# Turning queries and keys as plain fp32, two heads to a transpose, and splitting them after the turn

## The chip, the cores and the metric

The kernel runs on one core of one Trainium2 chip. The metric is the time of one execution on the device in microseconds (us). Each engine has its own queue of instructions and works it off in order: PE (TensorE) multiplies and transposes, DVE (VectorE), ACT (ScalarE) and POOL (GpSimd) work element by element, SP issues DMAs. PE writes into PSUM, which the other engines read.

## The reference, cut to what matters

512 tokens with 16 meta tokens ahead of them (528 in all, width 1024) pass through two layers. What the change touches is how queries and keys come about and who reads them: queries `q` (8 heads of 64, normalised), one key head `k`, and the same for the indexer, `q_idx` (8 heads of 64) and `k_idx`. The indexer's scores choose 128 keys for each query, and attention runs over those.

```python
def hybrid_layer(x, norm_g, w_in, qn_g, kn_g, ...):
    h = rms_norm(x, norm_g)
    proj = jnp.einsum('btd,de->bte', h, w_in)
    q, k, v, gate_a, u_b, gate_b, q_idx, k_idx, w_idx, merge = jnp.split(proj, ...)
    q = apply_rope(rms_norm(q.reshape(B, T, 8, 64), qn_g), cos_h, sin_h)
    k = apply_rope(rms_norm(k, kn_g), cos, sin)
    q_idx = apply_rope(q_idx.reshape(B, T, 8, 64), cos_h, sin_h)
    k_idx = apply_rope(k_idx, cos, sin)
    attn = indexer_sparse_attention(q, k, v, q_idx, k_idx, w_idx, k_top)
    y_a = jnp.einsum('bte,ed->btd', attn * jax.nn.silu(gate_a), w_a)
    ...                                   # a pooling branch y_b, two gates
    return x + jnp.einsum('btd,de->bte', g_a * y_a + g_b * y_b, w_out)

# indexer_sparse_attention, for one block of 128 queries
    s = jnp.einsum('bqhd,bkd->bqhk', qib, k_idx_f)
    score = jnp.einsum('bqhk,bqh->bqk', jax.nn.relu(s), wib * idx_scale)
    score = jnp.where(visible, score, NEG_INF)
    _, sel = lax.top_k(score, k_top)
    logits = jnp.einsum('bqhd,bqkd->bqhk', qb, gather(k, sel)) * attn_scale
    p = jax.nn.softmax(logits, axis=-1)
    out = jnp.einsum('bqhk,bqkd->bqhd', p, gather(v, sel))
```

## The kernel before, in words

**Precision.** Nearly every matmul keeps fp32's accuracy with operands in PE's faster fp32r format: an operand is split into a high part (the value rounded to fp32r, a CAST of ACT) and a low part (the value minus the high part, a subtraction of DVE), and the products of the parts are added up in PSUM. `hhi`/`hlo` are the split input, `w` holds the split weights. For queries and keys the two parts lie on the two halves of the partitions: `qi` (index queries) and `qq` (queries) are `[128, 4 heads, 128 tokens]` with a head's 64 high rows over (or under) its 64 low rows, and `KI` and `KK` are `[128, 2, 528]` with the key's high part doubled over all 128 partitions at index 0 and its low part at index 1, so that two matmuls (`a<-KI,qi`) give the whole product.

**Tiling.** Tokens are in one block of 16 (the meta tokens, t = 0) and four of 128 (t = 1 to 4). A projection of one token block to 256 columns (four heads) is a group of 24 matmuls 128x256, `tok_group`, into one PSUM bank `d`; it ends with `group_done()`. Two halves of eight heads make `g` = 0 and 1.

**Order.** The order of PE and DVE is the order in which the Python code emits instructions (a manual schedule); that of ACT, POOL and SP is set when the program is built. `later(fn, n)` runs `fn` n groups of PE work on. `half_done()` is called in the middle and at the end of each group and draws filler from generators: index scores (`index_steps`) and attention. A meter keeps estimated times of PE and DVE (`pe_cost`, `dve_cost`) and lets a step of the top-k search (`topk_steps`: 16 rounds of MAX8 and MATCH_REPLACE8 on score tiles `sc`) into DVE's order only when DVE is not ahead of its share; so an added DVE instruction moves the steps of the search to later places.

**PSUM.** Eight banks: three `d` for projections, four `a` for everything short (transposes, index scores, logits), one `v`. A bank is given out again in turn, and its next writer on PE waits until its last reader is done.

**Queries before the change** (`q_post`, 8 blocks of index queries and 8 of queries in each layer): two DVE products from PSUM (`t<-d,...`, L63 is the line of the meter's call, through which every PE and DVE instruction goes), POOL adds them (L677), ACT writes the high parts into `qs` (L686), DVE the low parts beside them (`qs<-t,qs`), PE turns `qs` by four fp32r transposes, one for a head with both parts (`a<-identr,qs`), and ACT copies the bank to `qi` or `qq` in one go (L697). The norm of the queries is applied later, in the softmax. The meta block's queries of layer 0 (t = 0) go the same way and stay as they are.

**Keys before the change** (`kv_post`, 5 blocks in each layer): four DVE products of 64 columns, POOL adds (L633), DVE scales by the norm (`t<-t,rk`), ACT writes the high parts twice into `ks` (L640), DVE the low parts (`ks<-t,ks`), four fp32r transposes, ACT copies to `KK` (L650) and `KI` (L651).

Of the kernel before, what the change touches and what calls it, by code (L numbers as in the profile page):

```python
# [9 lines left out]
F32R = mybir.dt.float32r  # L10
AF = mybir.ActivationFunctionType
OP = mybir.AluOpType
# [16 lines left out]
LB = 6  # L29
PB = 4  # L30
# [11 lines left out]
QN = 2  # L42
R_IDX = 3
UF = 2
QI = 3
# [46 lines left out]
def tile_block(ctx: ExitStack, tc: tile.TileContext, x, meta, w_in, pool_w, w_a, w_b, w_out, rows, hgain, c_tab, out):  # L92
    nc = tc.nc
    act, gp = nc.scalar, nc.gpsimd
    pe, dve = Metered(nc.tensor, pe_cost), Metered(nc.vector, dve_cost)
# [3 lines left out]
    tmp = ctx.enter_context(tc.tile_pool(name="tmp", bufs=2))  # L99
# [3 lines left out]
    def f(ap):  # L103
        return ap.bitcast(F32)
# [3 lines left out]
    def bank(tag, dt=F32):  # L108
        return psum.tile([128, 512], dt, tag=tag, name=tag, bufs=BANKS[tag])
# [229 lines left out]
    pend = deque()  # L339
# [4 lines left out]
    def later(fn, n=2):  # L344
        pend.append((count[0] + n, fn))
# [8 lines left out]
                    fill.popleft()  # L354

    credit = [0.0]

    sel = deque()
    spare, seen, share = [0.0], [0.0, 0.0], [FULL]

    def half_done():
        credit[0] += rate[0] / 2
        n = int(credit[0])
        credit[0] -= n
        pump(n)
# [22 lines left out]
        seen[1] = dve.us  # L388

    def flush():  # L390
        while pend:
            pend.popleft()[1]()

    def drain():
        while fill:
# [56 lines left out]
    KI = {}  # L452
# [151 lines left out]
    def kv_post(l, t, ps):  # L604
        s, m = TOK[t]
        p2 = ps[:m, :256].rearrange("p (g c) -> p g c", g=2)[:, :, 0:64]
        sq = tmp.tile([128, 64], F32, tag="tt", name="sq", bufs=6)
        ss = small(1, "ss")
        act.activation(sq[:m], ps[:m, 0:64], AF.Square, scale=HD ** -0.5, accum_out=ss[:m])
        rk = small(1, "rk")  # L610
        inv_rms(rk[:m], ss[:m])
        t1 = tmp.tile([128, HB], F32, tag="tt", name="t1", bufs=6)
        t2 = tmp.tile([128, HB], F32, tag="tt", name="t2", bufs=6)
        v1 = t1[:m, :128].rearrange("p (g d) -> p g d", g=2)
        for g, (C, S) in enumerate(((Cg, Sg), (ctab, stab))):
            dve.tensor_tensor(v1[:, g], p2[:, g], C[:m, t], op=OP.mult)
            dve.tensor_tensor(t2[:m, 64 * g:64 * g + 64].rearrange("p (a d) -> p a d", a=2),
                              p2[:, g].rearrange("p (a d) -> p a d", a=2)[:, ::-1, :],
                              S[:m, t].rearrange("p (a d) -> p a d", a=2), op=OP.mult)
        if t:  # L620
            act.activation(V[:, t - 1, :], ps[:, 64:128], AF.Copy, scale=0.5)
            act.activation(wab[:, t - 1], ps[:, 192:200], AF.Abs, scale=IDX_SCALE)
            act.activation(wsg[:, t - 1], ps[:, 192:200], AF.Sign, scale=-1.0 if t == 1 else 1.0)
        else:
            act.activation(VM, ps[:m, 64:128], AF.Copy, scale=0.5)

            def meta_values():
                rp = bank("a")
                pe.matmul(rp[:, :64], repl, VM, start=True, stop=True)
                for h in range(NH):  # L630
                    dve.tensor_scalar(BV[:, h // 2, h % 2, :], rp[:, :64], hmask[:, h:h + 1], None, op0=OP.mult)
            later(meta_values, 3)
        gp.tensor_tensor(t1[:m, :128], t1[:m, :128], t2[:m, :128], op=OP.add)  # L633
        ks = tmp.tile([128, 4, 128], F32R, tag="P", name="ks", bufs=PB)
        k4 = ks[:m].rearrange("p (g a) (b d) -> p g a b d", g=2, b=2)
        b1 = v1[:, :, None, :].to_broadcast([m, 2, 2, 64])

        def second():
            dve.tensor_scalar(t1[:m, :64], t1[:m, :64], rk[:m], None, op0=OP.mult)
            act.copy(k4[:, :, 0], b1)  # L640

        def third():
            dve.tensor_sub(k4[:, :, 1], b1, f(k4[:, :, 0]))

        def trans():
            tp = bank("a", F32R)
            for j in range(4):
                pe.transpose(tp[:, j * 128:j * 128 + m], ks[:m, j, :], identr[:m, :m])
            t4 = f(tp).rearrange("p (g j c) -> p g j c", g=2, j=2)
            act.copy(KK[:, :, s:s + m], t4[:, 0, :, :m])  # L650
            act.copy(KI[0][:, :, s:s + m], t4[:, 1, :, :m])  # L651
        later(second, 1)
        later(third, 2)
        later(trans, 4)

    def q_post(t, ps, normed, dst, g=0):
        s, m = TOK[t]
        p3 = ps[:m, :256].rearrange("p (h d) -> p h d", h=4)
        t1 = tmp.tile([128, HB], F32, tag="tt", name="t1", bufs=6)
        t2 = tmp.tile([128, HB], F32, tag="tt", name="t2", bufs=6)  # L660
        v1 = t1[:m, :256].rearrange("p (h d) -> p h d", h=4)
        C, S = (Cg[:m, t], Sg[:m, t]) if normed else (ctab[:m, t], stab[:m, t])
        dve.tensor_tensor(v1, p3, C[:, None, :].to_broadcast([m, 4, 64]), op=OP.mult)
        dve.tensor_tensor(t2[:m, :256].rearrange("p (h a d) -> p h a d", h=4, a=2), swapped(ps[:m, :256], 4),
                          S.rearrange("p (a d) -> p a d", a=2)[:, None, :, :].to_broadcast([m, 4, 2, 32]), op=OP.mult)
        if normed:
            sq = tmp.tile([128, HB], F32, tag="tt", name="sq", bufs=6)
            act.activation(sq[:m, :256], ps[:m, :256], AF.Square, scale=HD ** -0.5)
            ss = small(4, "ss4")
            rq = small(4, "rq")  # L670

        def norms():
            dve.tensor_reduce(ss[:m], sq[:m, :256].rearrange("p (h d) -> p h d", h=4), axis=AX.X, op=OP.add)
            inv_rms(rq[:m] if t == 0 else RQ[:, t - 1, 4 * g:4 * g + 4], ss[:m], gp if l else dve)
        if normed and t == 0:
            norms()
        added[0] = gp.tensor_tensor(t1[:m, :256], t1[:m, :256], t2[:m, :256], op=OP.add).ins  # L677
        if normed:
            qs = tmp.tile([128, 544], F32R, tag="L", name="qs", bufs=LB)[:, :512].rearrange("p (h c) -> p h c", h=4)
        else:  # L680
            qs = tmp.tile([128, 4, 128], F32R, tag="P", name="qs", bufs=PB)

        def second():
            if normed and t == 0:
                dve.tensor_tensor(v1, v1, rq[:m, :, None].to_broadcast([m, 4, 64]), op=OP.mult)
            act.copy(qs[:m, :, 0:64], v1)  # L686
            if normed and t:
                norms()

        def third():  # L690
            dve.tensor_sub(qs[:m, :, 64:128], v1, f(qs[:m, :, 0:64]))

        def trans():
            tp = bank("a", F32R)
            for h in range(4):
                pe.transpose(tp[:, h * 128:h * 128 + m], qs[:m, h, :], identr[:m, :m])
            act.copy(dst, f(tp).rearrange("p (h c) -> p h c", h=4)[:, :, :m])  # L697
        later(second, 1)
        later(third, QN if normed else QI)
        later(trans, QN + 1 + l if normed else QI + 1)  # L700

    SC = {}

    def index_steps(i, g, qS):
        n = NK[i]
        for hh in range(4):
            h = 4 * g + hh
            r = tmp.tile([128, 544], F32, tag="L", name="r", bufs=LB)
            for o, w in KPARTS[i]:
                ps = bank("a")  # L710
                pe.matmul(ps[:, :w], qS[:, hh, :], KI[0][:, 0, o:o + w], start=True, stop=False)
                pe.matmul(ps[:, :w], qS[:, hh, :], KI[0][:, 1, o:o + w], start=False, stop=True)
                e = min(w, n - o)
                act.activation(r[:, n - 1::-1] if i == 0 else r[:, o:o + e], ps[:, :e], AF.Relu,  # L714
                               scale=wab[:, i, h:h + 1])
            later(lambda h=h, r=r: accumulate(i, h, r), 1)
            yield
# [34 lines left out]
    QS = {}  # L752
# [4 lines left out]
    def attention(ensure, later_rate, on):  # L757
        st, pvs, pms, turned = {}, {}, {}, []

        def logits(u):  # L760
            i, j = divmod(u, 4)
            if j == 0:
                ensure(i)
                pms[i] = tmp.tile([128, NH, 16], F32, tag="pm", name="pm")
                if i == 0:
                    gp.tensor_scalar(NR, RQ, -1.0, None, op0=OP.mult)
            st[u] = []
            for hh in range(2):
                h = 2 * j + hh
                qS = QS[i, h // 4][:, h % 4, :]  # L770
                for pi, (o, w) in enumerate(KPARTS[i]):
                    ps = bank("a")
                    pe.matmul(ps[:, :w], qS, KK[:, 0, o:o + w], start=True, stop=False)
                    pe.matmul(ps[:, :w], qS, KK[:, 1, o:o + w], start=False, stop=True)
                    st[u].append((hh, pi, o, w, ps))
# [806 lines left out]
```

## Time and profile before

| | |
|---|---|
| runs (three) | 737.03, 737.45, 738.73 us; median 737.45 |
| span of the profiled execution | 735.6 us |
| around the span, taken as median less span | 1.85 us |
| PE busy | 730.1 us, 99% of the span |
| PE weight loads (overlap PE) | 706.0 us, 96% |
| DVE busy | 586.2 us, 80% |
| ACT busy | 482.1 us, 66% |
| POOL busy | 254.2 us, 35% |

The profiled execution's time is the span, from its first to its last instruction; the runs' times contain what lies around it. The page's forty slices show PE at nine tenths or more in all but the last, at a granted clock of nine tenths or more in all. The rows below have the form: engine and line, operation, output<-inputs by the program's names with buffer numbers left out, shape, count. A timeline's row begins with its start in the span and its length in us; a group's row ends with busy us, mean ns of one, and the idle time just before, with what ended most of it. Matmuls overlap, so the length of a PE row is longer than the time to the next row's start; prices of PE work are taken between starts.

### The profile page before, as it was taken

How to read it: one execution, taken by the hardware profiler on the slowest of the kernel's cores; microseconds unless marked ns; L12 is line 12 of the kernel's file. 1: busy time of each engine (PE TensorE's matmuls, PEld its weight loads, DVE VectorE, ACT ScalarE, POOL GpSimd, SP SyncE). 2: the span in 40 equal slices, each digit the busy share in tenths (PEclk: the TensorE clock that was granted, in tenths of full speed). 3: DMA queues.
4: the chain of work that ended last, by engine and by line, in shares of the span. 5: the costliest groups of instructions: out<-in, count | busy, mean ns of one | idle time of the engine just before them, and what ended most of it. 6: DMA issues, size and time to landing. Idle time of an engine off the chain costs nothing.

```text
span 735.6 us, 16083 instructions
## 1 busy us (share of the span) xinstructions
PE 730.1 (99%) x5949; PEld 706.0 (96%) x5949; DVE 586.2 (80%) x1478; ACT 482.1 (66%) x1099; POOL 254.2 (35%) x336
## 2 busy tenths in 40 slices
PE   9999999999999999999999999999999999999998
PEld 8999998999999999999999989998899999999997
DVE  6966999998997775894348668999989978768874
ACT  6779735757788886543245796357588977775643
POOL 3751174731222211163247411757131231106300
PEclk9999999999999999999999999999999999999999
DMA  8767765964655434643523778659564654438832
GB/s 268 233 172 165 167 145 115 229 149 99 141 119 122 94 84 105 192 141 118 143 89 87 171 175 199 157 116 205 126 156 103 144 115 90 113 107 268 202 88 71
DMA packets 103566, 106.41 MB, mean 145 GB/s; under 512 B 5008, under 2 KB 83632, under 8 KB 103488
## 3 DMA queue, kind: packets, MB, share of 16 engines
q1 hardware_dynamic: 91888, 74.89, 34.5%
q0 software_dynamic: 11520, 30.41, 23.1%
q8 instruction: 46, 0.75, 0.4%
q14 instruction: 32, 0.26, 0.1%
q10 hardware_dynamic: 80, 0.08, 0.0%
HBM read 66.41 MB, written 8.55 MB: 102 GB/s over the span
## 4 chain that ended last, share of the span: by engine, by line
PE 99%; DVE 0%; issue 0%; ACT 0%; DVEq 0%
PE d L63 80%; PE a L63 13%; PE v L63 5%; DVE ot L63 0%; DVE w L63 0%; ACT w L269 0%; ACT osum L1121 0%; DVE idle L63 0%; DVE nf L63 0%; DVE ta L63 0%; DVEq L63 0%; DVE ones L63 0%; ACT p L1021 0%; DVE ss L63 0%; DVE mhalf L63 0%
## 5 line engine op out<-in xcount | busy, mean ns | idle before, releaser
L63 PE MATMUL d<-hhi,w 128*128 128x256 f32 (+3 forms) x1392 | 278.4, 291 | 0.0
L63 PEld LDWEIGHTS d<-hhi,w 128*128 128x128 f32 x1392 | 222.2, 188 | 3.0 <-issue 0.6
L63 PE MATMUL d<-hlo,w 128*128 128x256 f32 (+3 forms) x696 | 189.8, 289 | 0.0
L63 DVE TENSOR_TENSOR w<-raw,w 128x512 fp32r<-128x512 f32 (+1 forms) x156 | 121.5, 785 | 14.0 <-ACT w L269 13.2
L63 PEld LDWEIGHTS d<-hlo,w 128*128 128x128 f32 x696 | 131.3, 189 | 1.4 <-issue 0.2
L63 PE MATMUL d<-hsum,w 128*128 128x264 f32 (+1 forms) x720 | 95.5, 285 | 0.0
L63 PEld LDWEIGHTS d<-hsum,w 128*128 128x128 f32 x720 | 89.6, 188 | 0.7 <-issue 0.3
L63 PE MATMUL d<-w,hhi 128*128 128x256 f32 x576 | 86.1, 287 | 0.0
L269 ACT CAST w<-raw 128x512 fp32r<-128x512 f32 x132 | 79.0, 624 | 6.7 <-DMA raw<-s 5.9
L63 PEld LDWEIGHTS d<-w,hhi 128*128 128x128 f32 x576 | 74.7, 188 | 4.7 <-issue 3.5
L255 POOL DMA_DIRECT2D raw<-raw x22 | 19.9, 905 | 115.5 <-DMA raw<-in_w_in_dram 30.3
L63 DVE MATCH_REPLACE8 sc<-m,sc 128x400 f32<-128x400 f32 (+2 forms) x100 | 54.4, 547 | 0.0
L221 POOL DMA_DIRECT2D w<-raw x34 | 31.8, 951 | 64.1 <-ACT w L220 46.5
L63 DVE MAX8 m<-sc 128x8 f32<-128x400 f32 (+2 forms) x100 | 53.2, 556 | 0.9
L793 ACT ACTIVATE lt<-lt,mn,NR 128x144 f32<-128x144 f32 (+3 forms) x64 | 42.3, 663 | 12.8 <-DVE mn L63 12.8
L284 POOL DMA_DIRECT2D raw<-s x22 | 19.6, 891 | 87.9 <-DVE s L63 40.7
L63 DVE SCALAR_TENSOR_TENSOR sc<-r,wsg,sc 128x144 f32<-128x144 f32 (+3 forms) x56 | 32.4, 582 | 16.9 <-ACT r L714 14.7
L63 PE MATMUL d<-w,hlo 128*128 128x256 f32 x288 | 45.6, 281 | 0.0
L63 PE MATMUL d<-mhi,w 128*128 128x272 f32 (+2 forms) x192 | 45.5, 324 | 0.0
L808 POOL TENSOR_SCALAR pm<-lt,rs 128x16 f32<-128x16 f32 x48 | 26.3, 575 | 44.2 <-DVE rs L63 33.1
L677 POOL TENSOR_TENSOR t<-t,t 128x256 f32<-128x256 f32 (+1 forms) x34 | 32.3, 951 | 25.6 <-DVE t L63 25.2
L1427 POOL TENSOR_TENSOR hlo<-ta,hhi 128x256 fp32r<-128x256 f32 (+1 forms) x28 | 26.8, 965 | 41.6 <-PE d L63 29.4
(247 smaller groups left out, 1564.5 us busy)
## 6 DMA issues: line engine op xcount, KB each, us to landing
raw<-in_w_in_dram SPq DMA_DIRECT2D x88, 256.0 KB, 3.5
w<-raw POOLq DMA_DIRECT2D x34, 512.0 KB, 5.9
raw<-in_w_in_dram SPq DMA_DIRECT2D x32, 512.0 KB, 4.6
raw<-in_w_out_dram SPq DMA_DIRECT2D x12, 512.0 KB, 3.8
raw<-raw POOLq DMA_DIRECT2D x22, 256.0 KB, 4.2
raw<-s POOLq DMA_DIRECT2D x22, 256.0 KB, 3.7
kept<-res SPq DMA_DIRECT2D x16, 264.0 KB, 3.2
res<-kept SPq DMA_DIRECT2D x16, 264.0 KB, 6.2
```

The source lines that it names most:

```text
L63: return fn(*a, **k)
L221: gp.dma_start(t, raws[c][s], accum_op=OP.add)
L255: gp.dma_start(raws[c][0][:, 1], raws[c][0][:, 0], accum_op=OP.add)
L269: act.copy(t[:, 0], blk[src[n]])
L284: gp.dma_start(blk["a12"], blk["s2"], accum_op=OP.add)
L677: added[0] = gp.tensor_tensor(t1[:m, :256], t1[:m, :256], t2[:m, :256], op=OP.add).ins
L793: act.activation(L[hh][:, :n], L[hh][:, :n], AF.Exp, scale=NR[:, i, h:h + 1], bias=mn[:, hh:hh + 1], accum_out=sm[:, hh:hh + 1])
L808: (gp if j < 3 else dve).tensor_scalar(pms[i][:, 2 * j + hh, :], L[hh][:, 0:16], rs[:, hh:hh + 1], None, op0=OP.mult)
L1427: pool_end = gp.tensor_sub(hlo[:, j, a:a + n], d, f(hhi[:, j, a:a + n]))
```

## The change

For the 16 query blocks a layer with t of at least 1, and for all key blocks, the split moves behind the transpose. The fp32 sum of POOL (`t1`) is turned by two fp32 transposes, each of 128 columns: two heads for queries; for keys, the key doubled in one and the index key doubled in the other (POOL now writes each twice, 256 columns instead of 128). ACT then casts the high parts from PSUM into their halves of `qi`/`qq` (two CASTs 64x256) or into `KK`/`KI` (two CASTs 128x128), and DVE subtracts them from the same bank and writes the low parts: for queries straight onto the other 64 partitions (two 64x256), for keys at index 1 (two 128x128). The low parts run two half groups after the transpose (`soon`). The bank is thus held until DVE has read it, not ACT.

Index queries are turned at `later(..., QI)`, one group earlier than before; queries and keys stay at theirs. Since a pair of heads (0 and 1, 2 and 3) comes out of one transpose, with the upper and lower half of the partitions, heads lie in `qi`/`qq` in the order 0, 2, 1, 3, and `place(h)` finds them. Heads 1 and 3 have their high rows on the lower half.

```diff
+    soon_q, ticks = deque(), [0]
+    def soon(fn):
+        soon_q.append((ticks[0] + 2, fn))
     def half_done():
+        ticks[0] += 1
+        while soon_q and soon_q[0][0] <= ticks[0]:
+            soon_q.popleft()[1]()
...
 # kv_post
-        gp.tensor_tensor(t1[:m, :128], t1[:m, :128], t2[:m, :128], op=OP.add)
...
+        gp.tensor_tensor(t1[:m, :256].rearrange("p (g b d) -> p g b d", g=2, b=2),
+                         *(v2[:, o, :, None, :].to_broadcast([m, 2, 2, 64]) for o in range(2)), op=OP.add)
         def second():
-            dve.tensor_scalar(t1[:m, :64], t1[:m, :64], rk[:m], None, op0=OP.mult)
-            act.copy(k4[:, :, 0], b1)
-        def third():
-            dve.tensor_sub(k4[:, :, 1], b1, f(k4[:, :, 0]))
+            dve.tensor_scalar(t1[:m, :128], t1[:m, :128], rk[:m], None, op0=OP.mult)
         def trans():
-            tp = bank("a", F32R)
-            for j in range(4):
-                pe.transpose(tp[:, j * 128:j * 128 + m], ks[:m, j, :], identr[:m, :m])
-            ...
-            act.copy(KK[:, :, s:s + m], t4[:, 0, :, :m])
-            act.copy(KI[0][:, :, s:s + m], t4[:, 1, :, :m])
+            tp = bank("a")
+            sides = [(g, K[:, 0, s:s + m], K[:, 1, s:s + m], tp[:, g * 128:g * 128 + m])
+                     for g, K in enumerate((KK, KI[0]))]
+            for g, hi, lo, p in sides:
+                pe.transpose(p, t1[:m, g * 128:g * 128 + 128], ident[:m, :m])
+            for g, hi, lo, p in sides:
+                act.copy(hi, p)
+            def low():
+                for g, hi, lo, p in sides:
+                    dve.tensor_sub(lo, p, f(hi))
+            soon(low)
         later(second, 1)
-        later(third, 2)
         later(trans, 4)
 # q_post
+        def paired():
+            tp = bank("a")
+            for b in range(2):
+                pe.transpose(tp[:, b * 128:(b + 1) * 128], t1[:, b * 128:(b + 1) * 128], ident)
+            own, other = slice(0, 64), slice(64, 128)
+            heads = [(dst[own, 0:2], dst[other, 0:2], tp[own]), (dst[other, 2:4], dst[own, 2:4], tp[other])]
+            heads = [(hi, lo, p[:, :256].rearrange("p (b c) -> p b c", b=2)) for hi, lo, p in heads]
+            for hi, lo, p in heads:
+                act.copy(hi, p)
+            def low():
+                for hi, lo, p in heads:
+                    dve.tensor_sub(lo, p, f(hi))
+            soon(low)
+        if t:
+            if normed:
+                later(norms, 1)
+            later(paired, QN + 1 + l if normed else QI)
+            return
...
+    def place(h):
+        return 2 * (h % 2) + h % 4 // 2
```

Three places show what moves. The first is PE in the index queries' part of layer 0, where `t_747` is the sum of POOL for one block of index queries; the difference of the two orders reads:

```order
 L63 MATMUL d<-hlo,w 128x272
 L63 MATMUL d<-hhi,w 128x272 x8
-L63 MATMUL a<-identr,qs 128x128 x4
+L63 MATMUL a<-consts,t_747 128x128 x2
 L63 MATMUL a<-KI,qi 128x400 x2
```

Four transposes of `qs` give way to two of the sum, against the identity matrix in `consts`, at the same place among the matmuls.

The second is PE a dozen matmuls behind that, where the scores of a later block of index queries take banks `a` in turn. Before (buffer numbers shown, and in brackets the counters that an instruction waits on):

```order
L63 MATMUL a_965<-KI_242,qi_609 128x272 [waits Activation_49]
L63 MATMUL a_965<-KI_242,qi_609 128x272
L63 MATMUL a_969<-KI_242,qi_609 128x256 [waits Activation_49]
L63 MATMUL a_969<-KI_242,qi_609 128x256
L63 MATMUL a_974<-KI_242,qi_609 128x272 [waits Activation_49]
L63 MATMUL a_974<-KI_242,qi_609 128x272
L63 MATMUL a_978<-KI_242,qi_609 128x256 [waits Activation_49]
```

And after:

```order
L63 MATMUL a_940<-KI_242,qi_592 128x272 [waits Activation_49]
L63 MATMUL a_940<-KI_242,qi_592 128x272
L63 MATMUL a_944<-KI_242,qi_592 128x256 [waits Activation_49]
L63 MATMUL a_944<-KI_242,qi_592 128x256
L63 MATMUL a_949<-KI_242,qi_592 128x272 [waits Activation_49]
L63 MATMUL a_949<-KI_242,qi_592 128x272
L63 MATMUL a_953<-KI_242,qi_592 128x256 [waits DVE_49,PE_49]
```

The fourth bank is the one that held the transposes; its next writer now waits for DVE (the low parts `qi<-a,qi`) where it waited for ACT's copy.

The third is DVE at the same place. Before, `qs<-t,qs` writes the low parts of a block ahead of its transposes:

```order
L63 SCALAR_TENSOR_TENSOR sc2_938<-r_911,wsg_134,sc2_938 128x400 [waits DVE_49,Activation_49]
L63 SCALAR_TENSOR_TENSOR silb_892<-th_928,d_893 128x272 [waits Activation_49]
L63 TENSOR_TENSOR qs_832<-t1_827,qs_832 128x4x64 [waits Pool_49]
L63 SCALAR_TENSOR_TENSOR sc2_938<-r_943,wsg_134,sc2_938 128x400 [waits DVE_49,Activation_49]
L63 TENSOR_SCALAR sc3_1004<-r_964,wsg_134 128x528 [waits Activation_49]
```

After:

```order
L63 SCALAR_TENSOR_TENSOR sc2_911<-r_887,wsg_134,sc2_911 128x400 [waits DVE_49,Activation_49]
L63 SCALAR_TENSOR_TENSOR silb_866<-th_904,d_867 128x272 [waits Activation_49]
L63 TENSOR_TENSOR qi_693<-a_906,qi_693 64x256 [waits PE_49,Activation_49]
L63 TENSOR_TENSOR qi_693<-a_906,qi_693 64x256
L63 SCALAR_TENSOR_TENSOR sc2_911<-r_916,wsg_134,sc2_911 128x400 [waits DVE_49,Activation_49]
L63 TENSOR_SCALAR sc3_977<-r_939,wsg_134 128x528 [waits Activation_49]
```

One subtraction of 256 columns from SBUF becomes two of 256 columns on 64 partitions each from PSUM, which stand behind the transposes instead of ahead of them, and behind the product of a gate (`silb<-th,d`).

Two things besides follow from the meter. The steps of the top-k search shift by some 76 matmuls, counted in PE's order without transposes: layer 0's last mask stands behind matmul 1535 instead of 1459 (first needed at 1627), layer 1's behind 4039 instead of 3963 (needed at 4067). PE's order is otherwise the same: 5203 matmuls that are no transposes in both, and 5547 in all instead of 5631.

More of the change, by code (lines that the diff above doesn't have):

```diff
@@ L390, in flush @@
     def flush():
-        while pend:
-            pend.popleft()[1]()
+        while pend or soon_q:
+            (soon_q if soon_q else pend).popleft()[1]()
     def drain():
@@ L613, in kv_post @@
         t2 = tmp.tile([128, HB], F32, tag="tt", name="t2", bufs=6)
-        v1 = t1[:m, :128].rearrange("p (g d) -> p g d", g=2)
+        v2 = t2[:m, :256].rearrange("p (o g d) -> p o g d", o=2, g=2)
         for g, (C, S) in enumerate(((Cg, Sg), (ctab, stab))):
-            dve.tensor_tensor(v1[:, g], p2[:, g], C[:m, t], op=OP.mult)
-            dve.tensor_tensor(t2[:m, 64 * g:64 * g + 64].rearrange("p (a d) -> p a d", a=2),
+            dve.tensor_tensor(v2[:, 0, g], p2[:, g], C[:m, t], op=OP.mult)
+            dve.tensor_tensor(v2[:, 1, g].rearrange("p (a d) -> p a d", a=2),
                               p2[:, g].rearrange("p (a d) -> p a d", a=2)[:, ::-1, :],
@@ L632, in kv_post @@
             later(meta_values, 3)
[L633 to L636, printed above, removed]
+        gp.tensor_tensor(t1[:m, :256].rearrange("p (g b d) -> p g b d", g=2, b=2),
+                         *(v2[:, o, :, None, :].to_broadcast([m, 2, 2, 64]) for o in range(2)), op=OP.add)
         def second():
-            dve.tensor_scalar(t1[:m, :64], t1[:m, :64], rk[:m], None, op0=OP.mult)
-            act.copy(k4[:, :, 0], b1)
-        def third():
-            dve.tensor_sub(k4[:, :, 1], b1, f(k4[:, :, 0]))
+            dve.tensor_scalar(t1[:m, :128], t1[:m, :128], rk[:m], None, op0=OP.mult)
         def trans():
-            tp = bank("a", F32R)
-            for j in range(4):
-                pe.transpose(tp[:, j * 128:j * 128 + m], ks[:m, j, :], identr[:m, :m])
-            t4 = f(tp).rearrange("p (g j c) -> p g j c", g=2, j=2)
-            act.copy(KK[:, :, s:s + m], t4[:, 0, :, :m])
-            act.copy(KI[0][:, :, s:s + m], t4[:, 1, :, :m])
+            tp = bank("a")
[9 more added lines that the diff above has]
+            soon(low)
         later(second, 1)
-        later(third, 2)
         later(trans, 4)
@@ L677, in q_post @@
         added[0] = gp.tensor_tensor(t1[:m, :256], t1[:m, :256], t2[:m, :256], op=OP.add).ins
[L678 to L681, printed above, removed]
+        def paired():
[16 more added lines that the diff above has]
+            return
+        qs = tmp.tile([128, 544], F32R, tag="L", name="qs", bufs=LB)[:, :512].rearrange("p (h c) -> p h c", h=4)
         def second():
-            if normed and t == 0:
-                dve.tensor_tensor(v1, v1, rq[:m, :, None].to_broadcast([m, 4, 64]), op=OP.mult)
+            dve.tensor_tensor(v1, v1, rq[:m, :, None].to_broadcast([m, 4, 64]), op=OP.mult)
             act.copy(qs[:m, :, 0:64], v1)
-            if normed and t:
-                norms()
         def third():
@@ L698, in q_post @@
         later(second, 1)
-        later(third, QN if normed else QI)
-        later(trans, QN + 1 + l if normed else QI + 1)
+        later(third, QN)
+        later(trans, QN + 1 + l)
+    def place(h):
+        return 2 * (h % 2) + h % 4 // 2
     SC = {}
@@ L710, in index_steps @@
                 ps = bank("a")
-                pe.matmul(ps[:, :w], qS[:, hh, :], KI[0][:, 0, o:o + w], start=True, stop=False)
-                pe.matmul(ps[:, :w], qS[:, hh, :], KI[0][:, 1, o:o + w], start=False, stop=True)
+                pe.matmul(ps[:, :w], qS[:, place(hh), :], KI[0][:, 0, o:o + w], start=True, stop=False)
+                pe.matmul(ps[:, :w], qS[:, place(hh), :], KI[0][:, 1, o:o + w], start=False, stop=True)
                 e = min(w, n - o)
@@ L769, in logits @@
                 h = 2 * j + hh
-                qS = QS[i, h // 4][:, h % 4, :]
+                qS = QS[i, h // 4][:, place(h), :]
                 for pi, (o, w) in enumerate(KPARTS[i]):
```

## The prediction

> **What bounds the kernel now.** I read the page's first part and its chain first, then PE's waits, then PE's groups and timeline, and DVE, ACT and POOL only where PE could come to wait for them.
>
> ```profile
> span 735.6 us, 16083 instructions
> PE 730.1 (99%) x5949; PEld 706.0 (96%) x5949; DVE 586.2 (80%) x1478; ACT 482.1 (66%) x1099; POOL 254.2 (35%) x336
> PE 99%; DVE 0%; issue 0%; ACT 0%; DVEq 0%
> ```
>
> The chain that ended last is PE for 99% of the span. The list of PE's waits (us in total, times, longest) has one entry:
>
> ```profile
> PE d L63 <- DVE ss L63: 1.5, 1, 1.5
> ```
>
> So PE hardly ever waits, and the time is the sum of PE's work. Whatever PE no longer does comes off the span, unless a wait takes its place. The three numbers to find are what the transposes cost PE, whether a new wait appears, and whether another engine becomes the bound. The profiled span is 735.6 us and the median of the three runs 737.45, so 1.85 us lie around the span; I work in the span and add that.
>
> **PE's gain.** The transposes that go are these (busy us, mean ns of one):
>
> ```profile
> L63 PE MATMUL a<-identr,qs 128*128 128x128 f32 x128 | 14.9, 240 | 0.0
> L63 PE MATMUL a<-identr,ks 128*128 128x128 f32 x32 | 3.8, 252 | 0.0
> L63 PE MATMUL a<-identr,ks 16*128 16x16 f32 x8 | 1.0, 224 | 0.0
> ```
>
> 128 of `qs` are 32 blocks, 32 of `ks` are 8 blocks, and the 8 small ones are the meta keys of two layers. The mean of 240 ns isn't their price, since they overlap. I take the price from periods: 24 matmuls 128x256 and one block of transposes, start to start. In layer 1's queries, where nothing else stands between (one period in full, then the next):
>
> ```profile
> 494.67 0.45 PE L63 MATMUL a<-identr,qs 128*128 128x128 f32 x4
> 494.96 1.18 PE L63 MATMUL d<-w,hhi 128*128 128x256 f32 x8
> 495.98 1.11 PE L63 MATMUL d<-w,hlo 128*128 128x256 f32 x8
> 496.93 1.11 PE L63 MATMUL d<-w,hhi 128*128 128x256 f32 x8
> 497.87 0.45 PE L63 MATMUL a<-identr,qs 128*128 128x128 f32 x4
> 501.08 0.46 PE L63 MATMUL a<-identr,qs 128*128 128x128 f32 x4
> ```
>
> 501.08 − 494.67 is 6.41 for two, 3.205 each. At the end of the kernel the same 24 matmuls stand with two fp32 transposes of `res` against the same `consts`, just what the change puts in; the first and the last of five such starts are:
>
> ```profile
> 688.03 0.38 PE L63 MATMUL a<-consts,res 128*128 128x128 f32 x2
> 700.25 0.38 PE L63 MATMUL a<-consts,res 128*128 128x128 f32 x2
> ```
>
> 12.22 for four, 3.055 each. A block of two fp32 transposes is thus 0.15 us cheaper than a block of four fp32r. Eight matmuls take 0.95 (496.93 less 495.98), 24 take 2.85, so the blocks cost about 0.35 and 0.20: an fp32 transpose takes a little longer than an fp32r one, but there are half as many. 40 blocks × 0.15 = 6.0 us. The meta keys' four transposes last from 402.33 to 402.74, 0.41:
>
> ```profile
> 402.33 0.47 PE L63 MATMUL a<-identr,ks 16*128 16x16 f32 x4
> 402.74 0.54 PE L63 MATMUL a<-identr,qs 128*128 128x128 f32 x4
> ```
>
> Half of that in two layers is 0.4. PE's sum falls by 6.4 us. The other 5203 matmuls stay, in their order.
>
> **DVE.** Its rows (the last is a pair on the timeline):
>
> ```profile
> L63 DVE TENSOR_TENSOR qs<-t,qs 128x256 fp32r<-128x256 f32 x32 | 16.1, 503 | 0.0
> L63 DVE TENSOR_TENSOR ks<-t,ks 128x256 fp32r<-128x256 f32 x8 | 4.9, 630 | 0.0
> L63 DVE TENSOR_TENSOR t<-d,consts 128x256 f32<-128x256 f32 x32 | 11.9, 412 | 2.9 <-PE d L63 2.9
> 44.24 0.75 DVE L63 TENSOR_TENSOR t<-d,consts 128x256 f32<-128x256 f32 x2
> ```
>
> A low part now is two TENSOR_TENSORs of 256 columns with one input in PSUM. The nearest row is `t<-d,consts`: 412 ns alone, two in a row 0.75. Nothing in the trace reads one half of the partitions and writes the other, so I bound the pair: 0.75 from below (the timeline's pair), 0.82 from above (two of 412 that don't overlap). I take 0.78. It replaces one of 503, so +0.28 × 32 = 9 us (8 to 10). The keys' one of 630 gives way to two of 128 columns; together as many columns, so I count it as nothing, between −0.3 and +0.1 a block; the scaling of 128 columns instead of 64 stands in the same bound. DVE goes from 586 to about 595 of some 730 us.
>
> On the whole span this fits. The stretch that has least room is the queries of layer 1 with the search beside them (us of 140: PE, PEld, DVE, ACT, POOL):
>
> ```profile
> 440.00:580.00 140.00, 140.00 (x1034) 131.27 (x1033) 134.12 (x347) 93.67 (x205) 58.30 (x79) 1.00 0.66 153
> ```
>
> DVE idles for 5.9 of 140. Its eight blocks add 8 × 0.28 = 2.2, at most 8 × 0.32 = 2.5, so it still fits. What absorbs it is the search: the meter puts its steps later, and nobody waits for them before the mask is read:
>
> ```profile
> 571.62 0.71 DVE L63 TENSOR_SCALAR sc<-sc 128x400 f32<-128x400 f32 x2
> 583.15 0.57 DVE L63 CUSTOM_DVE_ANT_0 lt<-a,sc 128x400 f32<-128x400 f32 x1
> ```
>
> The masks are done at 572.3 and first read at 583.15, 10.8 us later. The order moves them by 76 matmuls, at 0.95 / 8 = 0.12 each 9 us. That leaves some 2 us: no wait, though little is left. If that cover goes, attention's first DVE step is late, and behind it the `a` banks of its logits and PE.
>
> [...]
>
> **ACT and POOL.**
>
> ```profile
> L686 ACT CAST qs<-t 128x256 fp32r<-128x256 f32 x32 | 13.1, 408 | 16.9 <-POOL t L677 16.8
> L697 ACT CAST qq<-a 128x512 fp32r<-128x512 f32 x16 | 9.5, 592 | 1.6 <-PE a L63 1.6
> L633 POOL TENSOR_TENSOR t<-t,t 128x128 f32<-128x128 f32 x8 | 3.8, 484 | 0.1
> L677 POOL TENSOR_TENSOR t<-t,t 128x256 f32<-128x256 f32 x32 | 30.9, 965 | 20.0 <-DVE t L63 19.6 <-PE d L63 0.3
> ```
>
> ACT's 408 + 592 ns become two CASTs of 256 columns from PSUM at about 0.39 (the copy to `KI` below, the same columns, takes 0.38): −0.22 × 32 = −7 us, and its 16.8 us of waits for POOL go with L686. POOL's sum for keys doubles from 484 to the 965 of 256 columns, +0.5 × 8 = 4 us of its 254. Neither bounds anything: ACT was at 66%, POOL at 35%, and the keys' transposes come three groups (over 8 us) behind POOL's sum.
>
> **The new wait: the bank.** A bank of transposes was free when ACT had copied it; now it is free when DVE has subtracted, behind ACT and two half groups later at the earliest. In the changed order I counted, for each of the 42 blocks, PE's work between the transposes and the next writer of that bank: 5 to 25 us for the queries, 2.9 to 6.6 for most others, 2.5 at the tightest (a block of index queries, one in each layer). What DVE must do in the time shows before:
>
> ```profile
> 57.99 0.45 PE L63 MATMUL a<-identr,qs 128*128 128x128 f32 x4
> 58.29 1.05 ACT L225 CAST w<-raw 128x1024 fp32r<-128x1024 f32 x1
> 59.22 0.42 ACT L1290 ACTIVATE th<-d 128x272 f32<-128x272 f32 x1
> 59.51 0.60 ACT L697 CAST qi<-a 128x512 fp32r<-128x512 f32 x1
> 59.67 0.44 DVE L63 SCALAR_TENSOR_TENSOR silb<-th,d 128x272 f32<-128x272 f32 x1 [0.34 <-ACT th L1290]
> 60.14 1.14 PE L63 MATMUL a<-KI,qi 128*128 128x272 f32 x8
> ```
>
> The copy ends at 60.1, 2.1 after the transposes' start, since ACT is busy with a weight's cast. With two CASTs (0.7 together) it ends at about 60.2, and DVE's pair at 61.0. PE wants the bank at about 57.99 + 0.2 + 2.5 = 60.7: 0.3 late, up to 0.5. The other close place is the third key block:
>
> ```profile
> 42.69 0.46 PE L63 MATMUL a<-identr,ks 128*128 128x128 f32 x4
> 45.97 0.38 ACT L651 CAST KI<-a 128x256 fp32r<-128x256 f32 x1
> ```
>
> Its copies end at 46.35; DVE's pair follows with about 0.5, to 46.9. PE wants the bank 3.8 behind the transposes' end, at 46.7: 0.2 late, up to 0.9 if DVE has something else in front. Behind the waiting matmul stands all of PE, so each counts in full. Two such pairs, one in each layer: at least 0 (ACT may take the order otherwise), at most 2 × (0.5 + 0.9) = 2.8; I take 0.7, near the lower end, since the other 38 have more room than these delays.
>
> **Sum.** −6.0 − 0.4 + 0.7 = −5.7 us of 735.6, a span of 729.9; with 1.85 around it 731.8 us, 0.8% under the median.
>
> **Rivals.**
>
> 1. *The bank eats the gain.* If each of the 26 blocks of index queries and keys waited 0.2 us on average, 5.2 us came back and the time were about 737, within 0.2% of before (1.5 us, about what a measurement of this kernel can tell from no change). For it speaks that a step of the search takes over half a microsecond, and a low part behind two of them is 1.1 us late:
>
> ```profile
> L63 DVE MAX8 m<-sc 128x8 f32<-128x400 f32 (+2 forms) x100 | 53.2, 556 | 0.9
> ```
>
>    Against it: in those places most banks have 3 us and more, and few steps of the search can run while its scores are still being made. Here too belongs the case that the change doesn't do what it says, PE being paced by its weight loads (706 us) and not by the transposes; the two measured periods, with loads in both, speak against it.
> 2. *DVE becomes the bound* (slower). In 440 to 580 the low parts wait for ACT and hold DVE's queue, and the search with them, so that the masks come late. The point is where DVE adds more than its 5.9 us of idle there and the 2 us of cover that are left; the added cost is 2.5, and each of the eight blocks would have to hold DVE for 5.4 / 8 = 0.7 us more to get there. Then attention starts late in both layers. To end slower it must cost over 6.4 + 1.5 us, 4 in each layer: about 740. A block's CASTs have two half groups, 2.9 us, to be done in, so I think it unlikely.
> 3. [...] A plain fp32 matmul of 128 columns costs PE more:
>
> ```profile
> 239.19 1.16 PE L63 MATMUL v<-ptm,BV 128*128 128x128 f32 x8
> 240.19 0.82 PE L63 MATMUL a<-consts,lt 128*128 128x128 f32 x6
> ```
>
> Four matmuls (two records each) take 1.00, 0.25 each. At that price a block would cost 0.50 instead of 0.35, 40 × 0.15 = 6 us more than before: 743.5. The rows of `res` above, 0.20 for two, speak against it almost entirely. [...]
>
> **How the numbers follow.** The forecast gets 0.82, the first rival 0.11, the second 0.05, the third 0.02. The first is faster by over 0.2%, its own bounds (new waits of 0 to 2.8) being 731.0 and 733.9; two periods off by 0.02 × 40 move it by 0.8, to 730.2. The upper end goes to 736.2 to take in most of what lies between it and the first rival. Faster 0.82, same 0.11, slower 0.07.
>
> **What would show it.** Right: 84 fewer PE instructions (5865); `a<-consts,t` x2 in place of `a<-identr,qs` x4; periods of 3.06 at layer 1's queries; PE's waits under 3 us in all; DVE near 595, ACT near 475, POOL near 258; the masks of layer 1 done before the first `lt<-a,sc`. Wrong: PE waiting for DVE's `qi`, `KK` or `KI` many times (rival 1), DVE without idle time and PE waiting at the start of attention (2), or `a<-consts,t` pairs that take 0.5 (3).

## The result, and the profile after

The changed kernel takes 745.76 us (median of 744.77 to 746.34) against 737.5 before: 1.0109 times as long, 95% interval 1.0093 to 1.0124. The forecast was 731.8, faster. The first part of the page and its chain, after:

```profile
span 743.0 us, 15981 instructions
PE 727.7 (98%) x5865; PEld 700.7 (94%) x5865; DVE 603.0 (81%) x1520; ACT 475.1 (64%) x1089; POOL 254.5 (34%) x336
PE 72%; DVE 20%; issue 3%; ACT 3%; POOL 1%; DMA 1%; SPq 0%; DVEq 0%; ACTq 0%
```

PE's own work fell as it should (84 instructions fewer), but it is busy for 98% and the chain that ended last, 99% PE before, is now 72% PE and 20% DVE. PE's waits had one entry of 1.5 us; after, the list (us in total, times, longest) is:

```profile
PE d L63 <- ACT sq L673: 3.9, 3, 2.2
PE a L63 <- DVE KI L63: 3.1, 3, 1.2
PE d L63 <- DVE w L63: 2.4, 3, 1.7
PE d L63 <- DVE ss L63: 1.5, 1, 1.5
PE a L63 <- DVE qi L63: 0.2, 1, 0.2
PE a L63 <- DVE res L63: 0.2, 1, 0.2
```

Without the 1.5 us of `ss` and the last entry (at 8.90 us, ahead of all changed blocks), 9.6 us of this are new. The gain that the forecast rested on is there almost to the hundredth: in layer 1's queries the same 24 matmuls with a block of two fp32 transposes follow at

```profile
498.73 0.38 PE L63 MATMUL a<-consts,t 128*128 128x128 f32 x2
501.80 0.38 PE L63 MATMUL a<-consts,t 128*128 128x128 f32 x2
504.87 0.38 PE L63 MATMUL a<-consts,t 128*128 128x128 f32 x2
```

3.07 and 3.07 us, where 3.055 was forecast and 3.205 stood before. By these periods 40 × 0.135 + 0.4 = 5.8 us were won on the transposes (6.4 were forecast), the span is 743.0 − 735.6 = 7.4 longer, and so some 13 us were lost elsewhere. Set side by side, the starts of the same matmuls show where. The first of `d<-mhi,w` behind layer 0's queries stands at 143.17 before and 144.21 after; the next bank's first at 144.75 and 148.17.

**Layer 0's queries.** Timeline of DVE, ACT and PE there, after, in order of time:

```profile
142.93 0.42 DVE L63 TENSOR_TENSOR t<-d,Cg 128x256 f32<-128x256 f32 x1
143.26 0.41 DVE L63 TENSOR_TENSOR t<-d,Sg 128x256 f32<-128x256 f32 x1
143.77 0.38 ACT L673 ACTIVATE sq<-d 128x256 f32<-128x256 f32 x1 [0.19 <-DVE t L63]
144.21 0.39 PE L63 MATMUL d<-mhi,w 128*128 128x272 f32 x1 [0.86 <-ACT sq L673]
146.12 0.42 DVE L63 TENSOR_TENSOR t<-d,Cg 128x256 f32<-128x256 f32 x1
146.46 0.41 DVE L63 TENSOR_TENSOR t<-d,Sg 128x256 f32<-128x256 f32 x1
146.66 1.04 ACT L225 CAST w<-raw 128x1024 fp32r<-128x1024 f32 x1
147.73 0.39 ACT L673 ACTIVATE sq<-d 128x256 f32<-128x256 f32 x1
148.17 0.39 PE L63 MATMUL d<-mhi,w 128*128 128x256 f32 x1 [2.19 <-ACT sq L673]
```

DVE makes the two products of a block late: those at 142.93 belong to a bank whose group of matmuls had ended by 136.12 (the start of PE's next row), 6.8 us earlier; for the same block before, it was 139.66 and 135.78, 3.9. ACT's Square (`sq<-d`, for the norm) of the same bank starts only when DVE's second product is done (143.67, 143.77), and the bank `d` is free when the Square has ended. There are three banks `d`, each worth one group of 3 us, so PE comes back to a bank 6 us after it filled it: a lag of 4 us hides, one of over 6 with the Square behind it does not. The second time the Square also stands behind a weight's CAST on ACT (146.66). It is mostly DVE's lag that the name `ACT sq` in the waits hides.

DVE had no room there before. The windows of before (us of 20 in the order PE, PEld, DVE, ACT, POOL) are

```profile
120.00:140.00 20.00, 20.00 (x170) 18.00 (x169) 18.76 (x54) 11.36 (x24) 11.92 (x14) 1.00 0.66 158
140.00:160.00 20.00, 20.00 (x170) 19.85 (x169) 19.90 (x55) 14.15 (x31) 10.46 (x13) 1.00 0.95 226
```

18.8 and 19.9 us of 20 are DVE's.

**Layer 1's queries.** The same there (0.8 us of `ACT sq`), and after them DVE is late with the low parts of weights:

```profile
515.55 0.50 PE L63 MATMUL d<-mhi,w 128*128 128x512 f32 x1 [0.83 <-ACT sq L673]
539.00 4.51 PE L63 MATMUL d<-hsum,w 128*128 128x256 f32 x34 [1.73 <-DVE w L63]
```

The masks of layer 1, done 10.8 us ahead of their reader before, are now done 1.7 us ahead:

```profile
588.49 0.71 DVE L63 TENSOR_SCALAR sc<-sc 128x400 f32<-128x400 f32 x2
590.85 0.57 DVE L63 CUSTOM_DVE_ANT_0 lt<-a,sc 128x400 f32<-128x400 f32 x1
```

That is still in time, and the forecast had read it from the order (some 2 us left).

**Keys.** PE waits three times for low parts of keys. In layer 0 (DVE and PE):

```profile
39.03 1.22 DVE L63 TENSOR_TENSOR w<-raw,w 128x1024 fp32r<-128x1024 f32 x1
40.16 0.17 DVE L63 TENSOR_TENSOR KK<-a,KK 128x16 fp32r<-128x16 f32 x1
40.25 0.17 DVE L63 TENSOR_TENSOR KI<-a,KI 128x16 fp32r<-128x16 f32 x1
40.47 0.34 PE L63 MATMUL a<-KI,qi 128*128 128x144 f32 x1 [0.88 <-DVE KI L63]
```

The low parts of the 16 meta keys stand on DVE behind the low part of a weight (1.22 us), and the first index scores need them.

**What a block costs DVE.** After (a step of the search, the pair of low parts, the next instruction), and before (`qs<-t,qs` and the next):

```profile
508.23 0.56 DVE L63 MATCH_REPLACE8 sc<-m,sc 128x400 f32<-128x400 f32 x1
508.82 0.86 DVE L63 TENSOR_TENSOR qq<-a,qq 64x256 fp32r<-64x256 f32 x2
509.71 0.42 DVE L63 TENSOR_REDUCE ss<-sq 128x4 f32<-128x256 f32 x1
```
```profile
137.07 0.41 DVE L63 TENSOR_TENSOR qs<-t,qs 128x256 fp32r<-128x256 f32 x1
137.39 0.41 DVE L63 TENSOR_TENSOR t<-a,Cg 16x256 f32<-16x256 f32 x1
```

The pair holds DVE from 508.82 to 509.71, 0.89 us, and the step ahead of it doesn't overlap it (0.59 from its start to the pair's; 0.48 in two_ops below). That makes 1.0 us for a block, where this old subtraction held DVE for 0.32: 0.67 more. All 16 query blocks have 0.89 now, idle time behind it aside. Before, twelve had 0.32 to 0.37, but four had 0.67 to 1.21, 0.48 on the mean. So the added price is 0.67 for most and 0.5 on the mean, not 0.28.

### The profile page after: what moved, and what is told of

Its sections match the earlier page's. It is cut to its first block, busy times and chain, and to the rows that moved or that the text cites. A ratio compares the mean times of both kernels' runs of the same rounds, so it can differ in the third digit from the quotient of the medians.

```text
span 743.0 us, 15981 instructions
## 1 busy us (share of the span) xinstructions
PE 727.7 (98%) x5865; PEld 700.7 (94%) x5865; DVE 603.0 (81%) x1520; ACT 475.1 (64%) x1089; POOL 254.5 (34%) x336
## 4 chain that ended last, share of the span: by engine, by line
PE 72%; DVE 20%; issue 3%; ACT 3%; POOL 1%; DMA 1%; SPq 0%; DVEq 0%; ACTq 0%
PE d L63 58%; PE a L63 9%; DVE sc L63 4%; PE v L63 4%; DVE m L63 3%; DVE t L63 2%; DVE w L63 2%; DVE qq L63 1%; DVE mlo L63 1%; DMA xt<-in_x_dram 1%; DVE ss L63 1%; DVE silb L63 1%; DVE nf L63 1%; ACT w L225 0%; DVE us L63 0%
## 5 line engine op out<-in xcount | busy, mean ns | idle before, releaser
L736 ACT ACTIVATE r<-a,wab 128x272 f32<-128x272 f32 (+2 forms) x80 | 35.6, 489 | 13.1 <-PE a L63 12.8
L63 PEld LDWEIGHTS d<-mhi,w 128*128 128x128 f32 x192 | 33.1, 193 | 7.5 <-ACT sq L673 4.8
```

What stands on the lines that cost most here:

```text
L63: return fn(*a, **k)
```

## The experiments

Theory A: the low parts cost DVE some 0.5 to 0.67 us more for each block, and beside the queries DVE has no time left, so the banks `d` and the low parts of weights come late; the keys' low parts come late behind those of weights. Theory B: the longer hold of the banks `a` (the forecast's first rival). All kernels were timed beside the kernel before, on the same chip; ratios are to that.

**One part of the change at a time.** Three kernels change index queries, keys or queries alone and leave the other parts as before:

```diff
-        if t:
+        if t and not normed:      # iq_only;  "t and normed" in q_only, the old kv_post in both
             ...
             later(paired, QN + 1 + l if normed else QI)
             return
```

> Only the 16 blocks of index queries are changed; keys and queries go as before. Theory A (DVE's added time for the low parts is paid where DVE is already full, in the queries' parts, and late low parts of the keys cost the rest): DVE has idle time in the index queries' part, so 16 x 0.15 = 2.4 us come off and about 0.4 come back as a wait for a bank: about 735.5 us. Rival B (the longer hold of the banks a costs the time, everywhere that blocks are turned): this part has the tightest banks, so it should carry most of the loss: over 739.

> Only the key blocks are changed; index queries and queries go as before. Theory A: 8 x 0.15 + 0.4 = 1.6 us come off, and PE's waits for KI's low parts, which stand on DVE behind the low parts of weights (1.0 and 0.9 in layer 0, 1.2 in layer 1, in the changed kernel's waits), stay: about 739, PE's waits for KI about 3 us. Rival B: banks held longer, but by only five blocks a layer: about 737.

> Only the 16 query blocks (layer 0 and 1) are changed; keys and index queries go as before. Theory A: this carries most of the loss, since DVE has no idle time beside these blocks: 2.4 us come off, and about 5 in layer 0 (waits of 3 and a stretch of slower matmuls) and 4.5 in layer 1 come back: about 744.5. Rival B: the banks of these blocks have 5 to 25 us of room, so nothing is lost and 2.4 us come off: about 735.

| kernel | us | before | ratio (95%) |
|---|---|---|---|
| iq_only | 734.54 | 737.73 | 0.9958 (0.9946 to 0.9970) |
| keys_only | 738.25 | 737.73 | 1.0008 (0.9998 to 1.0018) |
| q_only | 744.99 | 737.73 | 1.0094 (1.0080 to 1.0109) |

Theory A met all three within 1 us. The part with the tightest banks `a` gains; the one whose banks have 5 to 25 us of room loses nearly all. The largest of PE's waits of q_only, then of keys_only (where about 3 us for KI were expected):

```profile
PE d L63 <- ACT sq L675: 3.8, 3, 2.2
PE d L63 <- DVE w L63: 2.4, 3, 1.7
```
```profile
PE a L63 <- DVE KI L63: 2.1, 2, 1.4
```

Theory B is out as the cause of the loss: no wait in q_only is for a bank `a`. (In the whole changed kernel two are, those at 36.30 and 62.03, 1.2 us.) The three parts sum to 4.6 us, the whole is 8.3, so some 3.7 come from their being together.

**The price of the low parts.** In one_op each block has one CAST and one subtraction, 128x256:

```diff
-            heads = [(dst[own, 0:2], dst[other, 0:2], tp[own]), (dst[other, 2:4], dst[own, 2:4], tp[other])]
+            heads = [(dst[:, 0:2], dst[:, 2:4], tp)]
```

> As the changed kernel, but for queries and index queries the two CASTs 64x256 are one of 128x256 and the two low parts are one subtraction of 128x256 on the partitions where the bank has them, so nothing is written across the halves; high parts of two heads then lie over one another and the products are not those of the heads. Same transposes, same places, same banks, same waits. Theory A: DVE's time for a block falls from about 0.95 to 0.41, the waits in the queries' parts go (about 8 us with the slow stretch), those for KI stay: 736 to 738. Rival C (it is the place of the low parts behind the transposes that stops DVE's queue, not their length): the waits stay, 743 to 746.

736.37 us, 0.9984 (0.9974 to 0.9994): at the same place behind the transposes, with the same wait for ACT's CAST, a shorter subtraction gives 9 us back. Rival C falls. Its low part, and the next instruction:

```profile
505.86 0.41 DVE L63 TENSOR_TENSOR qq<-a,qq 128x256 fp32r<-128x256 f32 x1
506.19 0.40 DVE L63 TENSOR_REDUCE ss<-sq 128x4 f32<-128x256 f32 x1
```

0.33 us, like most of the old ones. One wait of 1.5 us for the Square stays in layer 0, where ACT has CASTs of weights ahead of it.

two_ops issues that subtraction twice; two_cast does too, with ACT's CAST in two halves as in the changed kernel; own_half has both CASTs and both subtractions over one half of the partitions each, every one writing where it reads:

```diff
 # two_ops
+                    dve.tensor_sub(lo, p, f(hi))
                     dve.tensor_sub(lo, p, f(hi))
 # own_half
+                    dve.tensor_sub(lo[0:64], p[0:64], f(hi[0:64]))
+                    dve.tensor_sub(lo[64:128], p[64:128], f(hi[64:128]))
```

> As one_op, with its subtraction of 128x256 issued twice (the second writes the same low parts again): two instructions of the same length as the changed kernel's pair, charged the same by the meter, but none starts on other partitions than the one before. Theory A1 (much of the pair's added price is that an instruction which starts on other partitions waits for the end of the one ahead): a block takes about 0.75 us of DVE instead of 0.95, and PE's waits in the queries' parts shrink to a half: 739 to 742. Rival A2 (only the second instruction costs): as the changed kernel, 744 to 746.

> As two_ops, but the two CASTs and the two subtractions go over one half of the partitions each (64x256), each writing where it reads: lengths and count are those of the changed kernel, and DVE jumps to the other half and back in each block, but nothing is written across. Theory A1 (an instruction that starts on other partitions than the one ahead waits for that one's end): 0.9 us or a little more of DVE for a block, near the changed kernel: 743 to 745. Rival E (writing across the halves is what costs): as two_ops, 741.

> As own_half (two CASTs of one half each), but both subtractions go over all 128 partitions and 256 columns, as in two_ops: takes the jumps of DVE away and leaves ACT's work as in the changed kernel. Theory A1: 740 to 742, as two_ops. Rival F (two_ops was faster than the changed kernel because ACT had one CAST less): 744 to 746.

two_ops took 741.05 us, 1.0044 (1.0027 to 1.0061); two_cast 739.49, half a microsecond under its expected range, 1.0034 (1.0023 to 1.0045); own_half 744.76, 1.0095 (1.0081 to 1.0110). DVE in two_ops, then in own_half:

```profile
506.20 0.56 DVE L63 MATCH_REPLACE8 sc<-m,sc 128x400 f32<-128x400 f32 x1
506.68 0.87 DVE L63 TENSOR_TENSOR qq<-a,qq 128x256 fp32r<-128x256 f32 x2
507.47 0.41 DVE L63 TENSOR_REDUCE ss<-sq 128x4 f32<-128x256 f32 x1
```
```profile
506.44 0.56 DVE L63 MATCH_REPLACE8 sc<-m,sc 128x400 f32<-128x400 f32 x1
506.92 0.85 DVE L63 TENSOR_TENSOR qq<-a,qq 64x256 fp32r<-64x256 f32 x2
507.80 0.42 DVE L63 TENSOR_REDUCE ss<-sq 128x4 f32<-128x256 f32 x1
```

These rows stand for their kernels: over the 16 query blocks the pair's time varies by some 0.02 us. From its own start to the next one's the pair takes 0.79 us where it stays on the same partitions and 0.88 where it goes to the other half and back; the step ahead takes 0.48 in both. In the changed kernel these are 0.89 and 0.59. So the jumps between the halves cost 0.09 us a block in own_half and 0.21 in the changed kernel, where the first of the pair is held as well. Writing across adds little beyond that (rival E falls), and the number of ACT's CASTs does not matter (rival F falls). From one_op to the changed kernel 9.4 us are lost by the medians; about half comes with the second instruction (two_ops), the rest with the jumps. Why 0.1 us a block between two_cast and own_half is worth 5 us is settled only in part: 16 query blocks have only 1.6 us of it. Their profiles are 4.1 us apart, and by the starts of the same matmuls they part almost only beside the queries, by about 2 us in layer 0 and 1.9 in layer 1, in waits for the same banks and weights. In layer 0 the wait that takes 1.60 in two_cast takes 2.20 in own_half, and only there a stretch of slow matmuls follows (last section), about 1.1 us. How the tenths become so much in layer 1 stays open. The runs of own_half spread over 742.6 to 746.4, those of two_cast over 738.5 to 742.0.

**DVE without the search.** after_4 and before_4 have 4 rounds of the search instead of 16:

> The changed kernel with 4 rounds of the top-k search instead of 16 (fewer keys are chosen; everything behind works on the same shapes): some 20 us of DVE less in each layer, so that the search is over before the queries are projected and DVE has idle time beside them. Theory A (the loss in the queries' parts is DVE being full there): PE's waits in these parts go, about 8.5 us, those for KI stay: 736 to 738. Rival B (the low parts come late because they stand behind the transposes and ACT, whatever DVE has to do besides): 743 to 745.

> The kernel before with 4 rounds of the search instead of 16, as the reference for after_4. PE bounds it with or without the search, so theory A and rival B both expect 737 to 738.

after_4 took 736.55 us, 0.9984 (0.9974 to 0.9993); before_4 737.39, 0.9998 (0.9990 to 1.0007). With the same pairs, jumps and places, 9 us are gone as soon as DVE has time beside the queries; the same step takes nothing off the kernel before. PE's waits of after_4, but for two (0.6 us for `rstd`, which before_4 has too, and 0.2 for `qi`):

```profile
PE a L63 <- DVE KI L63: 3.2, 3, 1.7
PE d L63 <- DVE ss L63: 1.5, 1, 1.5
PE d L63 <- ACT zb L1408: 0.3, 1, 0.3
```

Those for the Square and the weights are gone, that for KI stays: the price of the pairs and the lack of room together make the loss.

**Moving the search.** meter charges what a pair costs above its estimate:

```diff
                     dve.tensor_sub(lo, p, f(hi))
+                dve.us += 0.3
             soon(low)
```

> The changed kernel with one line more: the meter is charged 0.3 us for each pair of low parts of queries and index queries, about what they take above its estimate, so that it puts steps of the search later. Nothing else changes. Theory A: in layer 0, where the masks are done 10 us before they are read, PE's waits of 3 us and the slow stretch go; in layer 1, where 1.7 us are left, little is won: 740 to 743. Rival D (DVE's sum of work in the stretch counts, not its order): 745 to 746.

744.71 us, 1.0095 (1.0078 to 1.0112): no gain that could be told from the changed kernel's 1.0109. Layer 0 has a wait of 2.5 us for the Square still. My expectation missed. But the added line moved little: between the products of the first and of the last query block, DVE's order has 12 steps of the search (each a MAX8 or a MATCH_REPLACE8) in layer 0, where the changed kernel has 13, and 17 in layer 1, where it has 19. So this doesn't decide whether moving more of the search would help (rival D).

**A version that is faster than both.** Index queries and keys changed, queries as before; and the same with the keys turned a group earlier:

```diff
         later(second, 1)
-        later(trans, 4)
+        later(trans, 3)           # iq_keys3
```

> Index queries and keys are changed, queries go as before. If the parts add up: 737.7 - 3.2 + 0.5 = 735. The three parts alone sum to 4.6 us above before and the whole is 8.3 above, so 3.7 come from their being together; if keys and index queries disturb one another (low parts of both on DVE, behind those of the weights), they show here: 738 to 739. If the rest comes from queries together with others, 735.

> As iq_keys, with the keys turned three groups behind their projection instead of four (the subtraction ahead of the transposes, which needed the group, is gone). Theory A: the low parts of the keys stand one group earlier on DVE and PE no longer waits for KI: 733, faster than either kernel. If the scaled sums are not ready a group earlier, PE waits for them instead: 735 to 738.

iq_keys took 737.67 us, 1.0000 (0.9990 to 1.0010); the sum of its parts would be 735.0, so index queries and keys disturb one another by 2.7 us of the 3.7 (PE waits 3.3 us for KI). iq_keys3 took 733.98, 0.9948 (0.9935 to 0.9962), half a per cent faster than before. PE's waits in it, but for 0.2 us for `qi`:

```profile
PE d L63 <- DVE ss L63: 1.5, 1, 1.5
PE a L63 <- POOL rstd L502: 0.9, 1, 0.9
PE a L63 <- DVE KI L63: 0.2, 1, 0.2
```

The wait for KI is down to 0.2 us. The wait of 0.9 us, at 22 us for POOL's first norm, isn't the change's: before_4, which differs from the kernel before only in the later search, has it too, with 0.7 at 22.15.

## Why the prediction was wrong, step by step

- *PE's gain, −6.4:* right, with 5.8 by the periods of 3.07. PE has 5865 instructions, and iq_only's 16 blocks gave 3.2 us, where 2.4 less 0.4 for a bank were expected.
- *DVE's term, +0.28 a block:* the first step that failed. It set the new pair's 0.78 against the old subtraction's mean length of 503 ns. But lengths overlap: from start to start the query blocks' old one took 0.32 to 0.37 in most and 0.48 on the mean, the pair 0.89 with 0.1 ahead of it: +0.5 on the mean, +0.67 in most. DVE was busy for 603.0 us where 595 was forecast. The forecast priced PE by periods for just this reason and did not do it for DVE. Its sum has nothing for the jumps between the halves either. The runs put these at 0.09 us a block in own_half (0.88 from the pair's start to the next one's, against 0.79 in two_ops) and at 0.21 in the changed kernel (0.89, with the step ahead held for 0.59 instead of 0.48).
- *"It still fits":* the second, and the deciding one. The forecast set eight blocks' 2.2 us against the 5.9 that DVE idles in 440 to 580. At the true price the eight cost 4.2 to 5.4, still under 5.9; but there is next to no idle time where they stand, beside layer 1's queries. Before the change (behind the comma stand PE, PEld and DVE):

```profile
480.00:500.00 20.00, 20.00 (x158) 18.55 (x158) 20.00 (x48) 11.63 (x20) 12.84 (x18) 1.00 0.64 139
500.00:520.00 20.00, 20.00 (x119) 17.16 (x118) 19.92 (x50) 15.30 (x30) 12.24 (x17) 1.00 0.95 217
```

Nor did the search give way there, on which the forecast counted: between the products of the first and the last query block, 19 of its steps stand in layer 1 before and after, and 15 and 13 in layer 0. So the added work made DVE late for the banks `d` and the weights of just this stretch. The query blocks suffice for that: q_only, with index queries as before, has the same waits (3.8 and 2.4 us). The forecast also took layer 1's stretch for the fullest and did not look at layer 0's queries, where DVE was at 18.8 and 19.9 of 20.

- *The wait that was searched for:* the forecast followed the banks `a` and gave them 0.7 us. The bank that stopped PE was `d`, freed by DVE's products and ACT's Square, 3.9 us by the waits; that an engine in arrears is late for all that stands in its queue was said of attention only.
- *Keys:* the forecast looked for a bank at the third key block, 0.2 to 0.9 us in each layer. None of the three waits is there. One, at 36.30, is for the bank of the first key block (1.0 us); two, at 40.47 and 411.84, are for the data, index scores that read the meta keys' low parts.
- *The rivals:* rival 2 (DVE becomes the bound, slower, about 740) named the right engine and direction, but not the path: its masks were in time, and PE waited beside the queries and not at the start of attention. It had 0.05 since its condition was reckoned with the 0.28 and the same 5.9 us. Rival 1 took 1.2 us in the waits (0.2 for `DVE qi`, 1.0 at 36.30). Rival 3 (transposes at the 0.25 us of a plain fp32 matmul) is refuted, by the same rows of 3.07.
- *ACT and POOL:* right for ACT (475); POOL stayed at 254.5 where 258 was forecast.

Of some 13 us lost, 9.6 are the new waits and some 1.3 the slow stretch below; the other 2 or so are not told apart (part of them is that a wait costs more than its entry: at 148.17 the same matmul falls back by 2.35 us against before, and 2.19 are listed).

## What to carry to other kernels

When work moves to another engine, price it there as on the bound one: from start to start among neighbours, with what it keeps the next one waiting, in the very windows where that engine is full, not over the span. A bound engine hides the arrears of another only as far as its buffers reach (here three banks, 6 us), so ask how many microseconds of lag the buffers between them are worth and how many the change adds. A change that pays in one place and costs in another is best made in the first alone: 0.9948 for index queries and keys, once the keys were turned a group earlier, 1.0109 for all.

## What the runs showed of the hardware that was not expected

PE was slower after a stall of 2.2 us. Behind the wait that ended at 148.17 the matmuls follow at 0.21 us instead of 0.12 for about 3 us, and the window's granted clock (the figure behind POOL's) is 0.62:

```profile
148.00:151.00 3.00, 2.83 (x16) 2.61 (x16) 2.90 (x8) 2.17 (x5) 2.10 (x4) 0.62 1.06 201
149.18 0.41 PE L63 MATMUL d<-mhi,w 128*128 128x256 f32 x1
149.39 0.41 PE L63 MATMUL d<-mlo,w 128*128 128x256 f32 x1
```

By the starts of the same matmuls this cost some 1.3 us. Behind the wait of 1.73 us at 539.00 it did not happen (34 matmuls in 4.51), but behind one of 1.71 at 38.01 in one_op it did (16 matmuls in 3.39 from 38.29 on, 0.21 each). The trace's record of the granted clock tells the two waits of the changed kernel apart: it reads 0.5 from 148.7 to 152.1, for 3.413 us, and 1.0 from 537.8 to 544.6. Besides, it reads 0.5 only from 742.6 on, behind the last matmul, and in the kernel before only from 734.2 on, behind the last one there. Cut the changed kernel's span, from 148.7 both ways, into pieces of 3.413: in the piece just ahead of 148.7 PE idles for 2.19 us. The wait at 539.00 lies across two pieces, with 0.6 us of it in one and 1.2 in the other, and in no other piece but those at the span's ends does PE idle for more than 1.2. That the idle time of such a piece decides is an estimate from these two waits; no run was made to show it.
